# Handing the last attention heads to the output gate in SBUF instead of through DRAM, in a two-layer encoder trunk on one core

## The chip, the core and the metric

The kernel runs on one core of one Trainium2 chip. Its engines work through queues of their own: PE (TensorE, matrix multiplies; its weight loads are listed as PEld), DVE (VectorE), ACT (ScalarE), POOL (GpSimd) and SP (SyncE, which here only issues DMAs; its rows in a timeline read SPq). Each engine takes its instructions in the order in which they were written, and waits for another engine or a DMA where the program put a semaphore. The metric is the device time of one execution in microseconds, as the median of several executions.

## The reference

An input x of 512 tokens by 1024 features goes through two layers. A layer normalizes x and projects it into queries, keys and values of its own mixer (8 heads of 128; in the first layer a dilated window attention with three dilations, in the second a grouped-query attention), queries of 4 memory heads, and a gate of 12 x 128 columns. The 12 head results are multiplied by the gate's SiLU and go through an output projection that is added to x:

```python
def reference(x, mem, ...):
    for i in range(DEPTH):                       # DEPTH = 2
        h = rmsnorm(x, norm_g[i])
        mem_h = rmsnorm(mem, mem_norm_g[i])
        if i % 2 == 0:
            proj = h @ w_in_a[j]
            o_mix = mixer_dilated(qkv, qn_a[j], kn_a[j], ang_a)          # 8 heads
        else:
            proj = h @ w_in_b[j]
            o_mix = mixer_axial_gqa(q, k, v, qn_b[j], kn_b[j], ang_b)    # 8 heads
        o_mem = memory_attention(q_mem, mem_h, w_mem_kv[i], ...)         # 4 heads
        o = concat([o_mix, o_mem])
        x = x + (o * silu(gate)) @ w_out[i]
```

## The kernel before

All matrix products work on split numbers: a weight piece of 128 x 1024 is loaded (`wl`, L246, issued by SP), in part summed with others by accumulating DMAs that POOL issues (L260 to L279), cast to its high part `wh` by ACT (L295) and to its low part `wo` by DVE (L305), and the products high x high, high x low and low x high go through PE at L170, L171 and L174 into the PSUM bank `pj`. Many of the large products are built from seven smaller ones (`s_chunk`): ACT or DVE takes each bank into a tile `sn` (L372 keeps it, L383 takes a difference, L389 adds), and finished quarters go to a caller's `ev`.

The order is written by a small driver. A "slot" passes with each chunk of weights; generators (attention heads, evacuations, preparations) are resumed when their slot is due, and each writes a few instructions into the engines' queues. The order on each engine is thus fixed when the program is built.

A finished head result is a tile `o` of 128 x 512 out of the pool `s2` (14 buffers that take turns). `attn_a` (first layer) and `attn_b` (second) hand it to `put_od` (L1002) or `put_ob` (L1295), which write it to the DRAM tile `od` or `odb` by a DMA on SP and note the head in `o_done`. `gates` makes the gate's columns with `s_chunk` in three groups: memory heads (g = 0), heads 0 to 3 (g = 1) and heads 4 to 7 (g = 2). Its `ev` gets a quarter: two heads by 256 tokens, 128 x 512. It writes the tanh (ACT), the SiLU's product (L787), waits for slots until both heads are in `o_done`, issues a load `og` of both heads' 256 tokens (L780), waits one more slot and multiplies: into `yf` at L795 (g < 2), or in place at L798 (g = 2). For g = 2 ACT then casts the high part of `y` (L801) and DVE takes the low part (L803), on which the products of `out_rest` work. Heads 6 and 7 make the last two quarters of each layer.

The output projection has a first part, again through `s_chunk`, whose results POOL adds to the residual with an accumulating DMA `acc<-sn` (L876, two halves), and a second part, `out_rest`, whose banks DVE adds to the same `acc` (L756), which hence waits for these DMAs. In the first layer the finished rows are then written to DRAM as `x1d` (L1254, SP) and normalized for the second layer (L482); the rotation tables `tbraw` and `grB` are loaded behind those writes in SP's queue (L1273, L1275) and used by DVE at L1279 and L1282. In the same stretch the memory tokens `m` of the second layer are normalized (ACT L475, POOL L477/L436/L437, DVE L482).

Of the kernel before, what the change touches and what calls it, by code (L numbers as in the profile page):

```python
# [13 lines left out]
ALU = mybir.AluOpType  # L14
# [10 lines left out]
BULK, ACTIVE, SET_AT, WARM, MEM_B, PREP_Y, ACC_AT, PREP_B, HALF, SET_B = 2, 2, 15, 1, 12, 1, 4, 1, {"a": 3, "b": 3, "o": 0}, 1  # L25
MEM_STEP = 1, 1
MEM_D = 4
PD = 2
EO = 2, 2, 1, 2, 2, 1
YB = {"m": (2, 2), "k": (1, 1, 1), 0: (1, 2, 1), 1: (1, 2, 1)}  # L30
# [95 lines left out]
def trunk_kernel(ctx: ExitStack, tc: tile.TileContext, x, mem, wall, norm_g, mem_norm_g, gcol,  # L126
                 qn_a, kn_a, qn_b, kn_b, ident_d, mask_d, tab_a, tab_b, out):
    nc = tc.nc
    V, A, G, T = nc.vector, nc.scalar, nc.gpsimd, nc.tensor
# [8 lines left out]
    def big(dt=F32, name="big"):  # L138
        return pool.tile([128, 2048], dt, tag="big", name=name, bufs=NBIG)

    def m4(dt=F32, name="m4"):
        return pool.tile([128, 1024], dt, tag="m4", name=name, bufs=NM4)

    def s2(dt=F32, name="s2"):
        return pool.tile([128, 512], dt, tag="s2", name=name, bufs=NS2)
# [321 lines left out]
    def norm_1(xb, both=False):  # L467

        ss = sm(2, "ss")
        for j in range(2):  # L470
            jk = s2(name="sq")
            if both and j:
                V.tensor_tensor_reduce(jk, xb[j], xb[j], 1.0 / 1024.0, 0.0, ALU.mult, ALU.add, ss[:, j:j + 1])
            else:
                A.activation(jk, xb[j], AF.Square, scale=1.0 / 32.0, accum_out=ss[:, j:j + 1])  # L475
        r, e = sm(1, "rstd"), sm(1, "mse")
        G.tensor_tensor(e, ss[:, 0:1], ss[:, 1:2], ALU.add)  # L477
        return rstd_of(e, 1)
# [113 lines left out]
    def halves(t):  # L592
        return [t[:, 0:512], t[:, 512:1024]]
# [17 lines left out]
    def mem_norm(layer):  # L611
# [4 lines left out]
        t = [halves(v) for v in t]  # L616
        yield MEM_D
        n = [norm_1(t[0])]
# [142 lines left out]
            chunk(1, 4, group, ev)  # L761


    def gates(od, o_done):

        ys, yf, y_done, YW = [None] * 4, [None, None], set(), {}

        def gate(H, first, g, half=False):


            yt = [[m4(F32R, "y").rearrange("p (h t) -> p h t", h=2) for _ in range(2)] for _ in range(2)] if g == 2 else None
            if g < 2:
                yf[g] = [m4(name="yf") for _ in range(2)]

            def ev(q, u, t):
                i, j = int(q[0]) - 1, int(q[1]) - 1
                h0, ts = first + 2 * j, slice(i * 256, (i + 1) * 256)
                def load():
                    o = s2(name="og")
                    nc.sync.dma_start(o.rearrange("p (h t) -> p h t", h=2), od[h0:h0 + 2, :, ts].rearrange("h p t -> p h t"))  # L780
                    return o

                o = load() if {h0, h0 + 1} <= o_done else None
                th = s2(name="th")
                A.activation(th, t, AF.Tanh, scale=0.5)
                yield 1
                V.scalar_tensor_tensor(t, th, 1.0, t, ALU.add, ALU.mult)  # L787
                yield 1
                if not o:
                    while not {h0, h0 + 1} <= o_done:  # L790
                        yield 1
                    o = load()
                    yield 1
                if g < 2:
                    V.tensor_tensor(yf[g][j][:, i * 512:(i + 1) * 512], t, o, ALU.mult)  # L795
                    y_done.add((g, i, j))
                    return
                V.tensor_tensor(t, t, o, ALU.mult)  # L798
                yield 1
                tv = t.rearrange("p (h t) -> p h t", h=2)  # L800
                A.copy(yt[j][0][:, :, ts], tv)  # L801
                yield 1
                V.tensor_tensor(yt[j][1][:, :, ts], tv, yt[j][0][:, :, ts].bitcast(F32), ALU.subtract)  # L803
                y_done.add((g, i, j))
                if {(2, 0, j), (2, 1, j)} <= y_done:
                    for k in range(2):
                        ys[2 * j + k] = (yt[j][0][:, k], yt[j][1][:, k])

            s_chunk(256, H, ev, tokens=False, half=half, soon=g == 2)

        def prep_y():

            def wait(*gi):
                while not {(g, i, j) for g, i in gi for j in range(2)} <= y_done:
                    yield 1

            def put(k, src):
                t = big(F32R, "y" + k)
                for j in range(2):
                    js = slice(j * 512, (j + 1) * 512)  # L820
                    lo = t[:, 1024 + j * 512:1024 + (j + 1) * 512]
                    A.copy(t[:, js], src[j])
                    V.tensor_tensor(lo, src[j], t[:, js].bitcast(F32), ALU.subtract)
                YW[k] = t.rearrange("p (a k t) -> p a k t", a=2, k=4)

            while None in yf:
                yield 1
            a11, a21, a12, a22 = [[yf[g][j][:, i * 512:(i + 1) * 512] for j in range(2)] for g in range(2) for i in range(2)]
            yield from wait((1, 0))
            put("12", a12)  # L830
            yield 1
            yield from wait((0, 0))
            put("11", a11)
            yield 1
            yield from wait((0, 1), (1, 1))
            s1 = [s2(name="ys") for _ in range(2)]
            for j in range(2):
                V.tensor_tensor(s1[j], a21[j], a22[j], ALU.subtract)
            yield 1
            put("S1", s1)  # L840
            yield 1
            for j in range(2):
                V.tensor_tensor(s1[j], s1[j], a11[j], ALU.subtract)
            yield 1
            put("S2", s1)
            yield 2
            for j in range(2):
                V.tensor_tensor(a12[j], a12[j], s1[j], ALU.add)
            yield 1
            put("S4", a12)  # L850
            yield 1
            for j in range(2):
                V.tensor_tensor(a21[j], a11[j], a21[j], ALU.subtract)
            yield 1
            put("S3", a21)
            yield 2
            put("22", a22)

        return gate, prep_y, YW, ys
# [52 lines left out]
    def prep():  # L912

        n = {}
        for c in range(5):
            if c < 4:
                n[c] = norm_1(xb[c])
            if c:
                norm_2(xb[c - 1], n[c - 1], rows["x"])
            if 1 < c < 4:  # L920
                first_t(H, xb[c - 2], c - 2)
            yield 1
        for c in range(2):
            yield from diffs_t(H, xb[2 + c], c)
            drv.spawn(rest_t(H, c, (2, 2, 2)), 1)
            yield 1

    def setup():

        nc.sync.dma_start(mask, mask_d)  # L930
        nc.sync.dma_start(tabA, tab_a.rearrange("p (b c d) -> p b c d", b=2, c=4))
        nc.sync.dma_start(grA[:, 0:3], qn_a[0:1, :, 0:32].to_broadcast([128, 3, 32]))
        nc.sync.dma_start(grA[:, 3:6], kn_a[0:1, :, 0:32].to_broadcast([128, 3, 32]))
        yield 4
        V.tensor_tensor(gk, gc[:, 0:3], gc[:, 3:6], ALU.mult)
        V.tensor_scalar(gk, gk, QS, None, ALU.mult)
        V.tensor_scalar(gc[:, 6:8], gc[:, 6:8], QS, None, ALU.mult)
        V.memset(gk[0:32, :], 1.0)
        V.tensor_scalar(grA[:, 0:3], grA[:, 0:3], QS, None, ALU.mult)
        yield 1  # L940
        for cs_ in range(2):
            G.tensor_tensor(ropeA[:, cs_], tabA[:, cs_, :, None, :].to_broadcast([128, 4, 6, 32]),
                            grA[:, None].to_broadcast([128, 4, 6, 32]), ALU.mult)
            yield 1
# [35 lines left out]

    drv.spawn(prep(), PD)
    drv.spawn(setup(), SET_AT)
# [11 lines left out]
    s_chunk(512, H, ev_v0)  # L994

    od = dram.tile([12, 128, S], F32, name="od", bufs=1)
    o_done = set()

    def put_od(i, t=None):
        if t is None:  # L1000
            return s2(name="o")
        nc.sync.dma_start(od[i], t)  # L1002
        o_done.add(i)

# [70 lines left out]
    def attn_a(h, qk0, qs, ks, v12, n_done):  # L1075
# [91 lines left out]

        pts = {}
        rs = put_od(h)

        def scale(o):
# [62 lines left out]
        pv(0)  # L1234
        yield 2
        put_od(h, rs)

    gate, prep_y, YW, ys = gates(od, o_done)
    for c in A_ORDER:
        if c.isdigit():  # L1240
            drv.later(attn_a(int(c), *head_chunk(int(c))))
# [45 lines left out]
    drv.spawn(setup_b(), SET_B)  # L1287

    od_b = dram.tile([12, 128, S], F32, name="odb", bufs=1)
    o_done_b = set()  # L1290

    def put_ob(i, t=None):
        if t is None:
            return s2(name="o")
        nc.sync.dma_start(od_b[i], t)  # L1295
        o_done_b.add(i)

# [142 lines left out]
    for kvh in range(2):  # L1440
# [9 lines left out]
        if kvh == 0:  # L1450
            drv.later(attn_b())

    gate, prep_y, YW, ys = gates(od_b, o_done_b)
    gate(H2, 8, 0, HALF.get("m"))
    gate(H2, 0, 1, HALF.get("a"))
    drv.spawn(prep_y(), PREP_B)
# [118 lines left out]
```

## Time and profile before

| | before |
|---|---|
| median of 3 runs | 966.98 us (965.21 to 967.11) |
| profiled execution | 968.3 us |
| its span, first to last instruction | 966.5 us |
| mean granted TensorE clock | 0.996 |
| PE busy | 946.8 us (98%) |
| DVE busy | 791.4 us (82%) |
| ACT busy | 681.7 us (71%) |
| POOL busy | 341.4 us (35%) |

The profile is of one execution, 1.8 us of which lie outside the span; it took 1.3 us more than the median. Starts are counted from the span's begin. In a timeline a row gives start, duration in all, engine, line, operation, output and input with their shape, how many instructions it stands for, and in brackets how long the engine was idle before it and what ended that. On DVE the durations of neighbours overlap, so the distance of two starts says more than the durations. The first layer ends and the second begins at about 590 to 690 us; the second layer's last gate lies at about 930 to 943 us.

### The profile page before, as it was taken

How to read it: one execution, taken by the hardware profiler on the slowest of the kernel's cores; microseconds unless marked ns; L12 is line 12 of the kernel's file. 1: busy time of each engine (PE TensorE's matmuls, PEld its weight loads, DVE VectorE, ACT ScalarE, POOL GpSimd, SP SyncE). 2: the span in 40 equal slices, each digit the busy share in tenths (PEclk: the TensorE clock that was granted, in tenths of full speed). 3: DMA queues.
4: the chain of work that ended last, by engine and by line, in shares of the span. 5: the costliest groups of instructions: out<-in, count | busy, mean ns of one | idle time of the engine just before them, and what ended most of it. 6: DMA issues, size and time to landing. Idle time of an engine off the chain costs nothing.

```text
span 966.5 us, 16604 instructions
## 1 busy us (share of the span) xinstructions
PE 946.8 (98%) x5682; PEld 833.2 (86%) x5682; DVE 791.4 (82%) x1411; ACT 681.7 (71%) x1701; POOL 341.4 (35%) x482
## 2 busy tenths in 40 slices
PE   8999999999999999999999999999899999999998
PEld 5879888888888888888899997788899999998886
DVE  5898676878888888888888999769878898769883
ACT  5775689686868686868685657546768977879770
POOL 1512423557554545454726011322332330111010
PEclk9999999999999999999999999999899999999999
DMA  9989956969686868685959889889766687777744
GB/s 360 317 235 327 271 116 172 294 120 268 149 258 143 262 150 258 154 261 132 283 132 241 266 206 297 268 242 366 167 157 129 199 235 179 207 204 190 206 131 131
DMA packets 89129, 209.81 MB, mean 217 GB/s; under 512 B 25298, under 2 KB 36050, under 8 KB 89044
## 3 DMA queue, kind: packets, MB, share of 16 engines
q1 hardware_dynamic: 69892, 145.76, 43.4%
q0 software_dynamic: 17856, 60.83, 33.4%
q10 hardware_dynamic: 1296, 2.16, 0.6%
q8 instruction: 45, 0.74, 0.3%
q14 instruction: 40, 0.33, 0.1%
HBM read 157.27 MB, written 12.65 MB: 176 GB/s over the span
## 4 chain that ended last, share of the span: by engine, by line
PE 80%; DVE 8%; DMA 6%; ACT 3%; issue 2%; POOL 1%; SPq 0%; DVEq 0%; POOLq 0%; ACTq 0%
PE pj L170 21%; PE pj L171 21%; PE pj L174 20%; DVE wo L305 2%; PE qT L585 2%; PE sa L1106 1%; PE oo L1208 1%; PE pt L1187 1%; PE sa L1102 1%; PE ptb L1405 1%; DMA og<-odb 1%; DMA acc<-sn 1%; DMA wl<-wl 1%; DMA grB<-in_qn_b_dram 1%; DMA od<-o 1%
## 5 line engine op out<-in xcount | busy, mean ns | idle before, releaser
L305 DVE TENSOR_TENSOR wo<-wl,wh 128x1024 fp32r<-128x1024 f32 x255 | 315.1, 1242 | 6.0 <-ACT wh L295 5.8
L295 ACT CAST wh<-wl 128x1024 fp32r<-128x1024 f32 x255 | 268.5, 1060 | 29.3 <-PE pj L171 18.9
L170 PE MATMUL pj<-wh,hS 128*128 128x512 f32 (+1 forms) x448 | 159.0, 368 | 3.9 <-DVE sn L389 3.9
L171 PE MATMUL pj<-wh,hS 128*128 128x512 f32 (+1 forms) x448 | 153.6, 356 | 0.0
L170 PE MATMUL pj<-wh,h 128*128 128x512 f32 (+1 forms) x336 | 117.9, 365 | 0.0
L171 PE MATMUL pj<-wh,h 128*128 128x512 f32 (+1 forms) x336 | 114.0, 353 | 0.0
L437 POOL TENSOR_TENSOR rstd<-mse,half 128x4 f32<-128x4 f32 (+2 forms) x98 | 103.1, 1052 | 8.2
L174 PE MATMUL pj<-wo,hS 128*128 128x512 f32 (+1 forms) x448 | 100.8, 355 | 2.0 <-DVE wo L305 2.0
L170 PEld LDWEIGHTS pj<-wh,hS 128*128 128x128 f32 x448 | 85.9, 192 | 14.8 <-issue 2.6
L171 PEld LDWEIGHTS pj<-wh,hS 128*128 128x128 f32 x448 | 86.1, 192 | 10.3
L372 ACT COPY sn<-pj 128x512 f32<-128x512 f32 x132 | 73.1, 590 | 29.7 <-PE pj L174 29.7
L436 POOL TENSOR_SCALAR mse<-hss 128x4 f32<-128x4 f32 (+1 forms) x86 | 45.1, 525 | 132.2 <-ACT junk L573 128.0
L174 PEld LDWEIGHTS pj<-wo,hS 128*128 128x128 f32 x448 | 75.3, 191 | 14.5 <-DVE wo L305 2.7
L573 ACT ACTIVATE junk<-sn 128x128 f32<-128x128 f32 x264 | 79.1, 308 | 4.1 <-DVE sn L383 4.1
L1050 POOL TENSOR_TENSOR ta<-sn,tabs 128x128 f32<-128x128 f32 (+1 forms) x64 | 37.4, 592 | 118.6 <-DVE sn L578 92.0
L389 DVE TENSOR_TENSOR sn<-pj,sn 128x512 f32<-128x512 f32 x99 | 67.7, 686 | 12.3 <-PE pj L174 11.8
L174 PE MATMUL pj<-wo,h 128*128 128x512 f32 (+1 forms) x336 | 74.8, 352 | 0.0
L171 PEld LDWEIGHTS pj<-wh,h 128*128 128x128 f32 x336 | 63.8, 190 | 7.4
L170 PEld LDWEIGHTS pj<-wh,h 128*128 128x128 f32 x336 | 63.6, 189 | 7.4 <-DVE sn L389 0.2
L279 POOL DMA_DIRECT2D wl<-wl x33 | 29.1, 881 | 111.9 <-DVE wo L305 56.0
L174 PEld LDWEIGHTS pj<-wo,h 128*128 128x128 f32 x336 | 56.0, 189 | 8.7
L578 DVE TENSOR_TENSOR sn<-sn,rstd 128x512 f32<-128x512 f32 (+1 forms) x82 | 48.0, 594 | 7.2 <-POOL rstd L437 7.2
(235 smaller groups left out, 2335.1 us busy)
## 6 DMA issues: line engine op xcount, KB each, us to landing
wl<-in_wall_dram SPq DMA_DIRECT2D x222, 512.0 KB, 7.0
wl<-wl POOLq DMA_DIRECT2D x66, 512.0 KB, 5.5
wl<-in_wall_dram POOLq DMA_DIRECT2D x42, 512.0 KB, 8.5
acc<-sn POOLq DMA_DIRECT2D x16, 256.0 KB, 4.8
od<-o SPq DMA_DIRECT2D x12, 256.0 KB, 5.6
og<-od SPq DMA_DIRECT2D x12, 256.0 KB, 5.5
odb<-o SPq DMA_DIRECT2D x12, 256.0 KB, 3.4
og<-odb SPq DMA_DIRECT2D x12, 256.0 KB, 4.2
```

The source lines that it names most:

```text
L170: T.matmul(o, a, b, start=start, stop=False, skip_group_check=True)
L171: T.matmul(o, c, d, start=False, stop=False, skip_group_check=True)
L174: T.matmul(o, a, b, start=False, stop=stop, skip_group_check=True)
L295: A.copy(wh, self.tile[self.items[i]])
L305: V.tensor_tensor(wo, self.tile[key], wh.bitcast(F32), ALU.subtract)
L372: A.copy(t, b)
L389: V.tensor_tensor(t, b, t, ALU.subtract if q == "12" else ALU.add)
L436: G.tensor_scalar(e, ss, EPS, None, ALU.add)
L437: G.tensor_tensor(r, e, half[:, 0:n], ALU.pow)
L573: A.activation(jk, p[:, j * 128:(j + 1) * 128], AF.Square, scale=QS, accum_out=ss[:, j:j + 1])
L578: V.tensor_tensor(xn[:, 0:n], p.rearrange("p (a b) -> p a b", a=4)[:, 0:n], r[:, 0:n, None].to_broadcast([128, n, 128]), ALU.mult)
L1050: G.tensor_tensor(ta[:, 0:n], xn[:, 0:n, 0:32], ropeA[:, 0, b, s0:s0 + n], ALU.mult)
```

## The change

The tile `o` of head 7 in the first layer and of heads 6 and 7 in the second is not written to DRAM. `put_od` and `put_ob` only note it in `o_here`, and the gate reads it from there. The gate's `ev` collects its two heads one by one: a head in `o_here` is taken as it is, and the partner of such a head that is in DRAM (head 6 of the first layer) gets a load of its own of 128 x 256. Where a quarter has such a head, the multiplication is made in two instructions, one for each head. A head that goes this way keeps its buffer of the pool until the multiplication.

```diff
+DIRECT, DIRECT_B = (7,), (6, 7)
...
-    def gates(od, o_done):
+    def gates(od, o_done, o_here, direct):
...
+                hs, got = (h0, h0 + 1), {}
+                tv = t.rearrange("p (h t) -> p h t", h=2)
                 def load():
-                    o = s2(name="og")
-                    nc.sync.dma_start(o.rearrange(...), od[h0:h0 + 2, :, ts]...)
-                    return o
-                o = load() if {h0, h0 + 1} <= o_done else None
+                    if "o" not in got and all(h in o_done for h in hs):
+                        ...                       # one load for both heads, as before
+                    for n, h in enumerate(hs):
+                        if h in got:
+                            continue
+                        if h in o_here:
+                            got[h] = o_here[h][:, None, ts].to_broadcast([128, 2, 256])
+                        elif h in o_done and (hs[1 - n] in direct):
+                            o = s2(name="og")[:, 0:256]
+                            nc.sync.dma_start(o, od[h, :, ts])
+                            got[h] = o[:, None, :].to_broadcast([128, 2, 256])
+                def times(dst):
+                    if "o" in got:
+                        V.tensor_tensor(dst, t, got["o"], ALU.mult)
+                    else:
+                        dv = dst.rearrange("p (h t) -> p h t", h=2)
+                        for n, h in enumerate(hs):
+                            V.tensor_tensor(dv[:, n], tv[:, n], got[h][:, n], ALU.mult)
+                load()
                 th = s2(name="th")
                 A.activation(th, t, AF.Tanh, scale=0.5)
...
-                if not o:
-                    while not {h0, h0 + 1} <= o_done:
+                if not all(h in got for h in hs):
+                    load()
+                    while not all(h in got for h in hs):
                         yield 1
-                    o = load()
-                    yield 1
+                        load()
+                    if not all(h in o_here for h in hs):
+                        yield 1
...
-                V.tensor_tensor(t, t, o, ALU.mult)
+                times(t)
...
     def put_od(i, t=None):
         if t is None:
             return s2(name="o")
+        if i in DIRECT:
+            o_here[i] = t
+            return
         nc.sync.dma_start(od[i], t)
         o_done.add(i)
...                                   # put_ob likewise, with DIRECT_B and o_here_b
```

The order on PE and on POOL stays as it was. In the changed kernel the lines behind the first of these edits have higher numbers: the load of both heads is at L785, that of one head at L794, the multiplication of both at L799, that of one at L803, the casts of `y` at L824 and L826, `put_od`'s write at L1028.

On DVE, at the end of the first layer (`o` is head 7's result, `og` what was loaded, `m` the memory tokens), this stands before:

```order
L1220 TENSOR_TENSOR o<-oo,o 128x512
L389 TENSOR_TENSOR sn<-pj,sn 128x512
L305 TENSOR_TENSOR wo<-wl,wh 128x1024
L389 TENSOR_TENSOR sn<-pj,sn 128x512
L305 TENSOR_TENSOR wo<-wl,wh 128x1024 x3
L798 TENSOR_TENSOR sn<-sn,og 128x512 x2
L383 TENSOR_TENSOR sn<-sn 128x512 x2
L803 TENSOR_TENSOR y<-sn,y 128x2x256 x2
L389 TENSOR_TENSOR sn<-pj,sn 128x512 x2
```

and this now:

```order
L1246 TENSOR_TENSOR o<-oo,o 128x512
L390 TENSOR_TENSOR sn<-pj,sn 128x512
L306 TENSOR_TENSOR wo<-wl,wh 128x1024
L390 TENSOR_TENSOR sn<-pj,sn 128x512
L306 TENSOR_TENSOR wo<-wl,wh 128x1024 x3
L803 TENSOR_TENSOR sn<-sn,og 128x256
L803 TENSOR_TENSOR sn<-sn,o 128x256
L803 TENSOR_TENSOR sn<-sn,og 128x256
L803 TENSOR_TENSOR sn<-sn,o 128x256
L384 TENSOR_TENSOR sn<-sn 128x512 x2
L826 TENSOR_TENSOR y<-sn,y 128x2x256 x2
L390 TENSOR_TENSOR sn<-pj,sn 128x512 x2
```

Nothing moved here: the two multiplications became four of half the width at the same place, and every other one of them reads head 7's tile itself.

On SP, in the last part of the first layer (`row` a norm's weights, `v` and `oth` pieces of the attention), this stands before:

```order
L1144 DMA oth<-ds 128x4x2
L598 DMA row<-in_norm_g_dram 128x1024
...
L780 DMA og<-od 128x2x256
L868 DMA acc<-in_x_dram 128x1024 x4
L246 DMA wl<-in_wall_dram 128x1024 x6
L598 DMA row<-in_mem_norm_g_dram 128x1024
L615 DMA m<-in_mem_dram 128x1024 x2
L1002 DMA od<-o 128x512
L246 DMA wl<-in_wall_dram 128x1024
L780 DMA og<-od 128x2x256 x2
L246 DMA wl<-in_wall_dram 128x1024 x8
L1254 DMA x1d<-acc 128x512 x4
```

and this now:

```order
L1170 DMA oth<-ds 128x4x2
L794 DMA og<-od 128x256
L599 DMA row<-in_norm_g_dram 128x1024
...
L794 DMA og<-od 128x256
L785 DMA og<-od 128x2x256
L891 DMA acc<-in_x_dram 128x1024 x4
L247 DMA wl<-in_wall_dram 128x1024 x6
L599 DMA row<-in_mem_norm_g_dram 128x1024
L616 DMA m<-in_mem_dram 128x1024 x2
L247 DMA wl<-in_wall_dram 128x1024 x9
L1280 DMA x1d<-acc 128x512 x4
```

The write of head 7 and the two loads of heads 6 and 7 are gone from between the weight loads, and two loads of head 6 alone stand some twenty rows further ahead, the first of them ahead of a norm's weights, the second ahead of the load of heads 4 and 5.

On DVE at the end of the second layer this stands before:

```order
L389 TENSOR_TENSOR sn<-pj,sn 128x512
L305 TENSOR_TENSOR wo<-wl,wh 128x1024 x2
L798 TENSOR_TENSOR sn<-sn,og 128x512 x2
L305 TENSOR_TENSOR wo<-wl,wh 128x1024
L383 TENSOR_TENSOR sn<-sn 128x512 x2
L803 TENSOR_TENSOR y<-sn,y 128x2x256 x2
```

and this now:

```order
L390 TENSOR_TENSOR sn<-pj,sn 128x512
L306 TENSOR_TENSOR wo<-wl,wh 128x1024
L803 TENSOR_TENSOR sn<-sn,o 128x256 x4
L306 TENSOR_TENSOR wo<-wl,wh 128x1024 x2
L826 TENSOR_TENSOR y<-sn,y 128x2x256 x2
L384 TENSOR_TENSOR sn<-sn 128x512 x2
```

Here both heads come from SBUF, no slot is waited for a load, and the four multiplications and the low parts of `y` stand one weight piece and one difference earlier. SP's two writes and two loads of this place are gone.

More of the change, by code (lines that the diff above doesn't have):

```diff
@@ L777, in ev @@
                 h0, ts = first + 2 * j, slice(i * 256, (i + 1) * 256)
+                hs, got = (h0, h0 + 1), {}
+                tv = t.rearrange("p (h t) -> p h t", h=2)
                 def load():
-                    o = s2(name="og")
-                    nc.sync.dma_start(o.rearrange("p (h t) -> p h t", h=2), od[h0:h0 + 2, :, ts].rearrange("h p t -> p h t"))
-                    return o
-                o = load() if {h0, h0 + 1} <= o_done else None
+                    if "o" not in got and all(h in o_done for h in hs):
+                        o = got["o"] = s2(name="og")
+                        nc.sync.dma_start(o.rearrange("p (h t) -> p h t", h=2), od[h0:h0 + 2, :, ts].rearrange("h p t -> p h t"))
+                        got[h0] = got[h0 + 1] = o.rearrange("p (h t) -> p h t", h=2)
+                    for n, h in enumerate(hs):
[15 more added lines that the diff above has]
+                load()
                 th = s2(name="th")
@@ L788, in ev @@
                 yield 1
-                if not o:
-                    while not {h0, h0 + 1} <= o_done:
+                if not all(h in got for h in hs):
+                    load()
+                    while not all(h in got for h in hs):
                         yield 1
-                    o = load()
-                    yield 1
+                        load()
+                    if not all(h in o_here for h in hs):
+                        yield 1
                 if g < 2:
-                    V.tensor_tensor(yf[g][j][:, i * 512:(i + 1) * 512], t, o, ALU.mult)
+                    times(yf[g][j][:, i * 512:(i + 1) * 512])
                     y_done.add((g, i, j))
                     return
-                V.tensor_tensor(t, t, o, ALU.mult)
+                times(t)
                 yield 1
-                tv = t.rearrange("p (h t) -> p h t", h=2)
                 A.copy(yt[j][0][:, :, ts], tv)
@@ L996, in trunk_kernel @@
     od = dram.tile([12, 128, S], F32, name="od", bufs=1)
-    o_done = set()
+    o_done, o_here = set(), {}
     def put_od(i, t=None):
@@ L1236, in attn_a @@
         put_od(h, rs)
-    gate, prep_y, YW, ys = gates(od, o_done)
+    gate, prep_y, YW, ys = gates(od, o_done, o_here, DIRECT)
     for c in A_ORDER:
@@ L1289, in trunk_kernel @@
     od_b = dram.tile([12, 128, S], F32, name="odb", bufs=1)
-    o_done_b = set()
+    o_done_b, o_here_b = set(), {}
     def put_ob(i, t=None):
@@ L1294, in put_ob @@
             return s2(name="o")
+        if i in DIRECT_B:
+            o_here_b[i] = t
+            return
         nc.sync.dma_start(od_b[i], t)
@@ L1451, in trunk_kernel @@
             drv.later(attn_b())
-    gate, prep_y, YW, ys = gates(od_b, o_done_b)
+    gate, prep_y, YW, ys = gates(od_b, o_done_b, o_here_b, DIRECT_B)
     gate(H2, 8, 0, HALF.get("m"))
```

## The prediction

> **What bounds the kernel now.** I read the page's busy times first, then what PE waits for, then the chain that ended last, and then the engines' timelines around PE's gaps.
>
> ```profile
> PE 946.8 (98%) x5682; PEld 833.2 (86%) x5682; DVE 791.4 (82%) x1411; ACT 681.7 (71%) x1701; POOL 341.4 (35%) x482
> ```
>
> PE is busy for 946.8 of 966.5 us. The change takes no matmul away, so it can gain only where PE stands still or runs at a low clock. PE's waits from 600 us to the end:
>
> ```profile
> PE pj L170 <- DVE sn L389: 3.2, 2, 2.5
> PE pj L174 <- DVE wo L305: 1.8, 1, 1.8
> PE xT L488 <- DVE acc L482: 1.3, 1, 1.3
> PE xT L488 <- issue: 0.7, 1, 0.7
> ```
>
> Here stand the total, the count and the longest. PE's timeline puts the three long ones, 1.3 + 1.8 + 2.5 = 5.6 us, into the start of the second layer, and DVE ends each:
>
> ```profile
> 664.57 1.06 PE L488 MATMUL xT<-ident,acc 128*128 128x128 f32 x8 [1.32 <-DVE acc L482]
> 681.56 1.22 PE L174 MATMUL pj<-wo,hS 128*128 128x256 f32 x8 [1.81 <-DVE wo L305]
> 685.25 0.55 PE L170 MATMUL pj<-wh,hS 128*128 128x256 f32 x1 [2.47 <-DVE sn L389]
> ```
>
> So from 664 to 685 us the kernel runs at DVE's pace. The chain says what DVE's pace hangs on: ahead of 650 us it goes through two DMAs, and from there by DVE nearly without a break to the last PE gap.
>
> ```profile
> 627.31 9.48 DMA acc<-sn
> ...
> 642.72 8.06 DMA grB<-in_qn_b_dram
> 684.50 0.61 DVE sn L389
> ```
>
> DVE's own timeline shows the same links, and ahead of them the wait that the change is about (in brackets the idle time before a row):
>
> ```profile
> 615.17 1.23 DVE L305 TENSOR_TENSOR wo<-wl,wh 128x1024 fp32r<-128x1024 f32 x1 [1.70 <-ACT wh L295]
> 618.25 1.38 DVE L798 TENSOR_TENSOR sn<-sn,og 128x512 f32<-128x512 f32 x2 [1.84 <-DMA og<-od]
> 619.54 1.29 DVE L383 TENSOR_TENSOR sn<-sn 128x512 f32<-128x512 f32 x2
> ...
> 636.89 0.69 DVE L756 TENSOR_TENSOR acc<-pj,acc 128x512 f32<-128x512 f32 x1 [3.21 <-DMA acc<-sn]
> ...
> 647.24 1.41 DVE L482 SCALAR_TENSOR_TENSOR acc<-acc,rstd,row 128x512 f32<-128x512 f32 x2
> 650.80 0.23 DVE L1279 TENSOR_SCALAR grB<-grB 128x128 f32<-128x128 f32 x1 [2.15 <-DMA grB<-in_qn_b_dram]
> ```
>
> **First layer: what the wait is worth.** SP issues the loads of heads 6 and 7 behind head 7's write:
>
> ```profile
> 613.51 1.37 SPq L780 DMA_DIRECT2D og<-od  x2
> 614.94 24.13 SPq L246 DMA_DIRECT2D wl<-in_wall_dram  x8
> ```
>
> In the changed kernel head 7 is in SBUF before DVE comes to the multiplication, and head 6's halves are loaded some 40 us ahead. DVE's wait of 1.84 us goes: the multiplications start at 618.25 - 1.84 = 616.41. What is late next there is DVE itself, since the `wo` piece at 615.17 had its own wait for ACT, which the change doesn't touch.
>
> The two multiplications of 128 x 512 take 619.54 - 618.25 = 1.29 us from start to start of the next group. Four of half the width replace them. The nearest rows for that width:
>
> ```profile
> L578 DVE TENSOR_TENSOR sn<-sn,rstd 128x256 f32<-128x256 f32 x32 | 12.7, 417 | 0.0
> 588.94 1.14 DVE L1174 TENSOR_SCALAR p<-p,c 128x256 f32<-128x256 f32 x4
> ```
>
> Four by 417 ns are 1.67 us if nothing overlaps; the four of L1174 took 1.14 us in all. So the split costs between 1.1 - 1.3 = -0.2 and 1.7 - 1.3 = +0.4 us. I take 0, the side of the four that ran in a row, which these will do too. [...]
>
> So DVE is done with the gate 1.8 us earlier. Both things behind it follow. POOL's accumulating DMAs wait for DVE's L383 and stand in POOL's queue around the memory tokens' norm, which waits for ACT, which waited for the multiplication:
>
> ```profile
> 618.97 1.30 ACT L801 CAST y<-sn 128x512 fp32r<-128x512 f32 x2 [2.53 <-DVE sn L798]
> 620.82 1.76 POOL L876 DMA_DIRECT2D acc<-sn  x2 [8.38 <-DVE sn L383]
> 626.65 1.85 POOL L876 DMA_DIRECT2D acc<-sn  x2
> ```
>
> The second pair at 626.65 moves to 624.8, and with it the landing at 627.31 + 9.48 = 636.79, DVE's L756 at 636.89, the `x1d` writes, the load of `grB` behind them in SP's queue, DVE at 650.80, and so PE's gaps: 1.8 us.
>
> One term can make it more. The last DMA of that pair took 9.48 us, and SP was issuing weight loads at the time (eight from 614.94 on, over 24 us). Put out earlier, it meets fewer of them, but it may also just wait for the same transfers: between nothing (or a little less than nothing) and several us. The cap comes from what is late next: if `grB` came sooner, DVE would still be at its L482 of 647.24 and free of it 2.15 us ahead of 650.80; that work moves only with PE's output, by the 0.7 us that PE waited (for "issue") in that stretch. Hence 2.15 + 0.7 = 2.85 us at most. Of the 1.0 us between 1.84 and that cap I take a little under half, 0.45 us, since I can't tell which end is nearer. The first layer's part is 1.84 + 0.45 = 2.3 us, with ends at 1.4 (split at its dearest, no relief) and 2.9.
>
> Nothing takes it back later: PE can follow, since its gaps of 5.6 us are more than twice as long, and the view of PE's waits has no DMA among its reasons after 600 us.
>
> **First layer: SP.** Head 7's write and two loads no longer stand among the weight loads. Those behind them may start earlier, but no PE wait names a weight load, so that is worth 0. If it did harm, it would be by taking DMA time from `acc<-sn`, which is in the term above. Head 6's two loads were moved the other way, and they are a rival below.
>
> **First layer: the pool.** Head 7's tile keeps its buffer until 617 us instead of the end of its write. The next taker comes out of the same 14 in turn, and the multiplication frees it earlier than it freed the `og` tiles before. Worth 0.
>
> **Second layer.** DVE's wait for the loads, 2.48 us, goes as well, and two writes and two loads. But here PE doesn't wait for DVE. From 912.6 us to the last instruction its only wait is this one, which ends right at the stretch's beginning, far ahead of this gate:
>
> ```profile
> PE pj L170 <- DVE sn L389: 0.7, 1, 0.7
> ```
>
> ```profile
> 937.72 1.37 DVE L798 TENSOR_TENSOR sn<-sn,og 128x512 f32<-128x512 f32 x2 [2.48 <-DMA og<-odb]
> ...
> 941.34 1.29 DVE L803 TENSOR_TENSOR y<-sn,y 128x512 fp32r<-128x512 f32 x2
> 942.46 1.07 PE L174 MATMUL pj<-wh,y 128*128 128x512 f32 x4
> ```
>
> PE comes to the low parts at 942.46, and DVE's first one is done by then. So this half of the change is worth 0, and its reordering can't cost either while DVE has 2.48 us to spare.
>
> **The sum.** 1.84 + 0.45 + 0 = 2.3 us: 968.3 - 2.3 = 966.0 us for an execution like the profiled one, which lay 1.3 us above the median, and 966.98 - 2.3 = **964.7 us** as the median.
>
> **The rivals.**
>
> The gain is swallowed. `acc<-sn` lands when the DMA engines are through with what is queued, not when it was issued, so the landing stays near 636.8, and the chain behind it too.
>
> ```profile
> acc<-sn POOLq DMA_DIRECT2D x16, 256.0 KB, 4.8
> ```
>
> For it: 9.48 us for 256 KB, beside weight loads; against it: the usual one of these DMAs lands in half that time. Time: 966.98, within 0.2%, which is 1.9 us and about what a measurement of this kernel can tell from no change.
>
> The clock changes phase. After the gap at 685.25 PE ran slowly for five microseconds:
>
> ```profile
> 685.60 0.41 PE L171 MATMUL pj<-wh,hS 128*128 128x256 f32 x1
> 685.81 0.41 PE L170 MATMUL pj<-wh,hS 128*128 128x256 f32 x1
> 690.46 0.28 PE L171 MATMUL pj<-wh,hS 128*128 128x256 f32 x1
> 690.58 0.29 PE L170 MATMUL pj<-wh,hS 128*128 128x256 f32 x1
> 685.00:691.00 6.00, 5.75 (x30) 5.78 (x31) 5.31 (x7) 2.66 (x11) 3.62 (x2) 0.57 0.35 115
> ```
>
> (The last row is a stretch: PE busy, PEld, DVE, ACT, POOL, then the granted clock, 0.57.) Starts were 0.21 us apart instead of 0.12, over 24 matmuls 24 x 0.09 = 2.2 us. With gaps that begin 2 us earlier or are shorter this can fall away: 2.3 + 2.2 = 4.5 us, 962.5. [...]
>
> Slower: head 6's early load holds SP up. The place is SP's queue at 567 us, behind `oth`:
>
> ```profile
> 567.06 3.30 SPq L598 DMA_DIRECT2D row<-in_norm_g_dram  x1
> ...
> 574.38 0.38 SPq L780 DMA_DIRECT2D og<-od  x1
> 561.86 7.57 DMA od<-o
> 588.34 0.69 DVE L798 TENSOR_TENSOR sn<-sn,og 128x512 f32<-128x512 f32 x1
> ```
>
> The load reads what head 6's write puts down, and that write lands at 561.86 + 7.57 = 569.43. SP, which would be at 567.06, waits 2.4 us, and behind it stand a norm's weights, weight loads, `v`, the load of heads 4 and 5 and four of `acc`; head 6's second half adds another 128 KB ahead of that load. The load of heads 4 and 5 is issued at 574.38, and at the 11.0 us that the DMA list gives as the median of this stretch it lands at 585.4, 2.9 us before DVE multiplies at 588.34.
>
> ```profile
> og<-od SPq DMA_DIRECT2D x2, 256.0 KB, 11.0
> 560.00:595.00 35.00, 33.32 (x199) 28.82 (x198) 34.16 (x55) 21.88 (x33) 5.98 (x7) 1.00 0.98 254
> ```
>
> The DMA engines are 98% busy there (next to last number) and DVE 34.16 of 35 us, so a later landing has no cover beyond these 2.9 us. The shift is from 0 (SP's 3.3 us for `row` may be the same waiting) to 2.4 us and the time of head 6's 256 KB at 254 GB/s, 1.0 us: 3.4. That would stall DVE 0.5 us and leave a gain of 1.8. For a loss the landing must come over 2.9 + 2.3 = 5.2 us later, by weight and `acc` loads that overtake it; each us beyond that is a us lost. At twice my upper shift, 6.8 us, it is 1.6 us slower: 968.6.
>
> That the second layer's part, half of the change, does nothing is my forecast already.
>
> **How the numbers follow.** Forecast (gain 1.4 to 2.9): 0.53, of which 0.10 ends within 0.2%. Clock: 0.12. Swallowed, or cut below 1.9 us by SP: 0.20. Slower: 0.15, of which 0.02 stays within 0.2%. Faster 0.43 + 0.12 = 0.55; same 0.10 + 0.20 + 0.02 = 0.32; slower 0.13. The range leaves out about a tenth on each side: from 962.4, which takes in the clock case's 962.5, to 967.8, halfway from no change to the slower rival's 968.6.
>
> **What would show it.** Right: no DVE wait for `og` in the first layer, `acc<-sn` of the second pair issued near 624.8 and landed near 634.5, `grB` used near 648.5, PE's last gap ending near 683. Wrong: the issue earlier but the landing at 636.8 (swallowed); a DVE wait for the load of heads 4 and 5 near 588 (slower); no low clock behind the last gap (clock); a second-layer tail that is longer or shorter than before.

## The result

The changed kernel takes 964.9 us (median of 22 runs, 962.83 to 968.33), the kernel before 967.24 us in the same comparison (22 runs). The ratio is 0.9969, 95% interval 0.9959 to 0.998: a gain of 3.0 us, between 1.9 and 4.0. By the medians it is 2.3 us, by the means 2.9: the kernel before has more long executions, two of them above 972 us, and a median doesn't see these. Disturbed runs, of which the experiments below have one of 1978.12 us in `e5` and one of 1032.56 us of the kernel before beside `e5` to `e8`, are left out of the ratios and not of the medians. The forecast was 2.3 us and 964.7 us.

### The profile page after: what moved, and what is told of

Same layout as the page of the kernel before. It is cut to its first block, busy times and chain, and to the rows that moved or that the text cites. A ratio compares the mean times of both kernels' runs of the same rounds, so it can differ in the third digit from the quotient of the medians.

```text
span 963.8 us, 16603 instructions
## 1 busy us (share of the span) xinstructions
PE 946.6 (98%) x5682; PEld 834.1 (87%) x5682; DVE 791.4 (82%) x1415; ACT 681.9 (71%) x1701; POOL 343.0 (36%) x482
## 4 chain that ended last, share of the span: by engine, by line
PE 84%; DVE 8%; DMA 4%; ACT 3%; issue 2%; DVEq 0%; ACTq 0%
PE pj L171 22%; PE pj L172 22%; PE pj L175 22%; DVE wo L306 2%; PE qT L586 2%; PE oo L1234 1%; PE sa L1132 1%; PE pt L1213 1%; PE sa L1128 1%; PE ptb L1434 1%; DMA og<-odb 1%; DMA x1d<-acc 1%; DMA od<-o 1%; PE row L607 1%; PE ob L175 1%
## 5 line engine op out<-in xcount | busy, mean ns | idle before, releaser
L172 PEld LDWEIGHTS pj<-wh,hS 128*128 128x128 f32 x448 | 86.1, 192 | 10.2
```

Of the source, the lines that this page charges most:

```text
L172: T.matmul(o, c, d, start=False, stop=False, skip_group_check=True)
```

## The profile after

Its span is 963.8 us against 966.5. Of PE's waits from 600 us to the end these are left (total, count, longest):

```profile
PE pj L171 <- DVE sn L390: 3.0, 2, 2.5
PE pj L175 <- DVE wo L306: 1.1, 1, 1.1
PE ob L175 <- DVE pbT L1443: 0.6, 1, 0.6
```

Gone are the wait of 1.3 us for `acc` at 664 us, and the two of 0.7 and 0.2 us for "issue" and for the low part of `y`, which lay right behind the gate. The DVE timeline at the gate and at the links behind it:

```profile
589.82 0.69 DVE L799 TENSOR_TENSOR sn<-sn,og 128x512 f32<-128x512 f32 x1
...
616.66 1.23 DVE L306 TENSOR_TENSOR wo<-wl,wh 128x1024 fp32r<-128x1024 f32 x1 [1.72 <-ACT wh L296]
617.80 0.42 DVE L803 TENSOR_TENSOR sn<-sn,og 128x256 f32<-128x256 f32 x1
618.13 0.42 DVE L803 TENSOR_TENSOR sn<-sn,o 128x256 f32<-128x256 f32 x1
...
619.14 1.29 DVE L384 TENSOR_TENSOR sn<-sn 128x512 f32<-128x512 f32 x2
...
636.16 0.69 DVE L757 TENSOR_TENSOR acc<-pj,acc 128x512 f32<-128x512 f32 x1 [3.03 <-DMA acc<-sn]
...
644.04 0.69 DVE L757 TENSOR_TENSOR acc<-pj,acc 128x512 f32<-128x512 f32 x1 [2.03 <-PE pj L175]
...
648.32 0.22 DVE L1305 TENSOR_SCALAR grB<-grB 128x128 f32<-128x128 f32 x1
```

The first row says how the two executions must be laid side by side: the same instruction stood at 588.34 before. This execution was thus 1.5 us late when it came to the place of the change, for reasons that lie ahead of it. From there on it gained: the multiplications start 0.45 us earlier than before by the clock of the span, so 1.9 us by this measure; `acc` of L757 is taken 0.7 us earlier (2.2); `grB` is used 2.5 us earlier (4.0), with no wait in brackets. POOL's second pair of accumulating DMAs:

```profile
626.25 1.85 POOL L899 DMA_DIRECT2D acc<-sn  x2
```

And SP at the place of the slower rival, then the DMA list for the stretch in which the load of heads 4 and 5 is issued:

```profile
568.39 0.85 SPq L1170 DMA_DIRECT2D oth<-ds  x1
574.23 0.32 SPq L794 DMA_DIRECT2D og<-od  x1
...
580.11 0.54 SPq L785 DMA_DIRECT2D og<-od  x1
```

```profile
og<-od SPq DMA_DIRECT2D x1, 256.0 KB, 9.2
```

SP stood from 569.24 to 574.23, 5.0 us, and what ended that was head 6's write. The load of heads 4 and 5 was issued at 580.11 and took 9.2 us: 589.3, half a microsecond before DVE used it at 589.82, without a wait.

## The experiments

Three questions: which half of the change works, and by which of its effects; by which path the gain reaches the end; what the early loads and the second layer take from it. Ratios are to the kernel before, each with its 95% interval.

### Which half

`e1_first_only`:

```diff
-DIRECT, DIRECT_B = (7,), (6, 7)
+DIRECT, DIRECT_B = (7,), ()
```

> The changed kernel with the first layer's half alone: DIRECT = (7,), DIRECT_B = (). Theory (the whole gain is the first layer's, since PE never waits for DVE in the second layer's last gate): as the changed kernel, 2.3 to 3 us under the kernel before, about 964.5 us. Rival (the second layer's wait of 2.48 us on DVE also counts): the gain splits, this run lies 1 us or more above the changed kernel, about 966. Profile: no DVE wait for og near 617 us, the wait for odb of about 2.5 us near 935 us back, PE without a gap there.

Measured: 964.97 us, ratio 0.9972 (0.9958 to 0.9986), the whole gain as far as these runs can tell. At the second layer's last gate (925 to 950 us) DVE waits for `odb` again:

```profile
DVE sn L799 <- DMA og<-odb: 2.7, 1, 2.7
```

`e2_second_only`:

```diff
-DIRECT, DIRECT_B = (7,), (6, 7)
+DIRECT, DIRECT_B = (), (6, 7)
```

> The changed kernel with the second layer's half alone: DIRECT = (), DIRECT_B = (6, 7). Theory: no change, 966.5 to 967.5 us, with DVE's wait for odb near 935 us gone and PE's tail as long as before. Rival (the second layer counts): 1 us or more faster than before, about 966 or less.

Measured: ratio 1.0008 (0.9993 to 1.0022), so between 0.7 us faster and 2.1 us slower than the kernel before. The median, 969.1 us, lies above the 966.5 to 967.5 that were expected; why is open. The rival, a gain of 1 us or more, is out: the second layer's half brings nothing. A wait of 2.5 us on DVE was taken away where PE had work.

This run showed something else, which the kernel before's profile had hidden. In its first layer, which is that of the kernel before, DVE's timeline reads:

```profile
620.02 1.38 DVE L799 TENSOR_TENSOR sn<-sn,og 128x512 f32<-128x512 f32 x2 [2.68 <-DMA og<-od]
...
646.06 0.69 DVE L757 TENSOR_TENSOR acc<-pj,acc 128x512 f32<-128x512 f32 x1 [2.03 <-PE pj L175]
...
650.35 0.22 DVE L1305 TENSOR_SCALAR grB<-grB 128x128 f32<-128x128 f32 x1
```

and PE's, right behind the gate:

```profile
621.42 0.50 PE L171 MATMUL pj<-wh,y 128*128 128x512 f32 x1 [0.60 <-ACT y L824]
...
623.25 0.73 PE L175 MATMUL pj<-wh,y 128*128 128x512 f32 x2 [0.17 <-DVE y L826]
...
627.46 0.63 PE L489 MATMUL xT<-ident,m 128*128 128x128 f32 x4 [0.73 <-issue]
```

Here DVE doesn't wait for `grB` at all. It waits 2.03 us for PE's last bank of `out_rest`, and PE is late because it had itself waited 0.60 + 0.17 + 0.73 = 1.5 us for what comes out of the gate. The wait of 2.03 us is no sign of this execution: it stands there in all fourteen profiles, the kernel before's at 644.29. So DVE comes to this bank ahead of PE in all of them, and behind it the gate can be felt only through PE or through a DMA.

How late PE is can be read between two groups of its matmuls, the one that begins at 617.91 in the kernel before and the last of `out_rest`; first the kernel before, then the changed one:

```profile
617.91 1.07 PE L174 MATMUL pj<-wo,y 128*128 128x512 f32 x4
...
643.18 1.07 PE L174 MATMUL pj<-wh,y 128*128 128x512 f32 x4
```

```profile
619.39 1.07 PE L175 MATMUL pj<-wo,y 128*128 128x512 f32 x4
...
642.94 1.07 PE L175 MATMUL pj<-wh,y 128*128 128x512 f32 x4
```

That is 25.27 and 23.55 us. The same distance in the five profiles in which the first layer's gate waits for its load `og`, and in the nine in which it doesn't (e4, e9 and e10 come further down):

| profile | DVE's wait for `og`, us | PE from group to group, us | more than 23.55 |
|---|---|---|---|
| before | 1.84 | 25.27 | 1.72 |
| e4 | 1.91 | 25.33 | 1.78 |
| e10 (two waits) | 2.42 | 25.87 | 2.32 |
| e9 | 2.65 | 26.13 | 2.58 |
| e2 | 2.68 | 26.11 | 2.56 |
| the nine others | none | 23.54 to 23.55 | 0 |

PE thus loses DVE's wait, less about 0.1 us, in every one of these executions, the kernel before's among them. The brackets show only part of it (0.20 + 0.69 in the kernel before), as it counts from the listed end of a matmul (these start 0.23 us apart and are listed with 0.39), and as the first ones behind a stand took longer: from L488's eight matmuls at 625.69 to the next group it was 1.09 us, in the changed kernel 0.79.

There are then two paths from the gate to PE's later gaps: this one, straight through PE, and the predicted one by way of `grB`, which is the last only where `grB` lands late.

### Which effect

`e3_traffic_kept` is `e1` with head 7's write and both loads of heads 6 and 7 issued at their old place as well, into tiles that nobody reads, so that DVE doesn't wait for them. Head 6's two early loads are there too:

```diff
         if i in DIRECT:
             o_here[i] = t
+            nc.sync.dma_start(od[i], t)
             return
...
+                    if any(h in direct for h in hs):
+                        spare = s2(name="spare")
+                        nc.sync.dma_start(spare..., od[h0:h0 + 2, :, ts]...)      # read by nobody
```

> First layer's half alone, but head 7 is also written to DRAM and both loads of heads 6 and 7 are still issued at their old place, into tiles that nobody reads; SP's queue there is that of the kernel before, only DVE doesn't wait for it. (Head 6's two early loads are there too.) Theory (it is DVE's wait that counts): as with the first layer's half alone, about 964.5 us. Rival (what counts is that SP's queue and the DMA engines are rid of the write and the loads, so that weight loads run ahead and acc<-sn and grB land sooner): the gain falls to 1 us or less, 966 us or more; in between, the part of each can be read from the landing of acc<-sn and from whether DVE waits for grB.

Measured: 964.66 us, ratio 0.9967 (0.9951 to 0.9983). The whole gain is there, with the write and both loads in SP's queue at their old place:

```profile
609.88 0.33 SPq L1030 DMA_DIRECT2D od<-o  x1
610.25 0.42 SPq L247 DMA_DIRECT2D wl<-in_wall_dram  x1
614.61 1.57 SPq L818 DMA_DIRECT2D spare<-od  x2
```

```profile
617.31 0.42 DVE L803 TENSOR_TENSOR sn<-sn,og 128x256 f32<-128x256 f32 x1
...
635.96 0.69 DVE L757 TENSOR_TENSOR acc<-pj,acc 128x512 f32<-128x512 f32 x1 [3.06 <-DMA acc<-sn]
```

So it is DVE's wait, and neither the traffic nor the weight loads behind it. POOL's second pair stood at 625.77 here, and the last of it was used 635.96 - 625.77 = 10.2 us later. That distance is 10.2 us in the kernel before as well (626.65 to 636.89), and 9.9 us in the changed one (626.25 to 636.16), without the traffic.

### By which path

`e4_tables_early` and `e5_after_tables_early` load the tables early, in the kernel before and in the changed one:

```diff
+    def tables():
+        if not tabs_b:
+            ...                                       # tbraw, grB and their loads, moved here
     def ev_o(n, b, x1):
+        if (n, b) == (0, 2):
+            tables()
         if n:
```

> The kernel before, with the loads of grB and tbraw issued ahead of the first x1d writes in SP's queue instead of behind them (about 3.5 us sooner). Theory (the last link ahead of PE's gaps is DVE's wait for grB, 2.15 us, behind which DVE is free at 648.65): that wait goes, DVE still waits 1.8 us for og, and the kernel is about 2 us faster, 965. Rival (grB's wait is no link, what is late next comes at the same time, such as the L482 that waits for acc): 967, as before.

Measured: 966.35 us, ratio 0.9986 (0.9973 to 1.0): 0.9 us by the medians and 1.4 by the ratio, of the 2 us that were expected, and the interval reaches to no gain. DVE takes `grB` without a wait, at about the time of e2, and the wait for `og` and PE's waits behind the gate are still there:

```profile
650.11 0.22 DVE L1289 TENSOR_SCALAR grB<-grB 128x128 f32<-128x128 f32 x1
```

> The changed kernel with grB and tbraw loaded early as in e4: the fourth corner of a square with the kernel before, the changed kernel and e4, where grB is out of the way in both. Theory A, as predicted (the gain came through acc<-sn, x1d and grB to DVE): with grB early that path is cut, and this run should lie where e4 lies, 966.4. Theory B, formed from the profiles of e2 and e4 (DVE didn't wait for grB there, but for PE's banks of out_rest; what the change closes are PE's own waits for the gate at 621 to 627 us, 0.60 + 0.17 + 0.73 = 1.5 us): 1.5 to 1.9 us under e4, 964.5 to 964.9, and about 0.9 us under the changed kernel or equal to it.

Measured: 966.33 us, ratio 0.9978 (0.9963 to 0.9993). That alone speaks for neither theory: the median is e4's, as theory A had it, the ratio lies between, and without its longest execution the median is 966.04 us. Its profile shows why it can't decide. PE's wait from 900 us to the end:

```profile
PE pj L171 <- DVE sn L390: 3.2, 1, 3.2
```

That wait, 0.7 us before and 0.5 us in the changed kernel, stands where DVE waits for the load of heads 4 and 5 of the second layer, which still go through DRAM. In this execution what was gained in the first layer was lost there.

So the square was repeated without that place. `e8_four_heads_second`, `e9_no_first_four_second`, `e10_tables_four_second` and `e11_tables_first_four_second` all have

```diff
+DIRECT, DIRECT_B = (7,), (4, 5, 6, 7)      # e8; e11 with the tables early
+DIRECT, DIRECT_B = (), (4, 5, 6, 7)        # e9; e10 with the tables early
```

> The changed kernel with heads 4 to 7 of the second layer handed over, DIRECT_B = (4, 5, 6, 7). PE's wait near 910 us (0.5 to 0.7 us, for a sum that stands behind the multiplication by heads 4 and 5 on DVE) should go with the wait for their load: 0.5 us faster than the changed kernel, 964.3. Rival: DVE is full there anyway and the wait stays, 964.9; or two more buffers held make the attention wait, 966 or more.

> DIRECT = (), DIRECT_B = (4, 5, 6, 7): the first layer as before, heads 4 to 7 of the second layer handed over in SBUF. It is e8 without the first layer's half, so that the second wait for a way through DRAM (heads 4 and 5 of the second layer, PE idle 0.2 to 3.2 us near 910 in the profiles so far) can't take anything back. Theory: 0.5 us under the kernel before, 966.7, and 1.5 to 2.5 us over e8, with PE's waits for the gate at 621 to 627 us (0.9 to 1.5 us in all) still there. Rival (the first layer's gain only shows because of the second layer's wait): e8's time, 964.6.

> As e9, with grB and tbraw loaded early: no late grB, no wait near 910; only the first layer's gate still waits for DRAM. Theory B: 0 to 1 us under e9, about 966; DVE's wait of 1.8 to 2.7 us for og near 617 us and PE's short waits behind it still there. Theory A (the predicted path through acc<-sn and grB is the only one): as e11.

> As e10, with the first layer's half of the change: e5 without the wait near 910 us. If e5 lost its gain there (3.15 us of PE in its profile), this run is 1.5 to 2 us under e10 and about 1.5 to 2 under e5, 964 to 964.5. If it lies at e10's time, the first layer's half works only through grB, and theory B falls. It is also the first candidate for a version faster than the changed kernel (964.9).

| heads 4 to 7 of the second layer in SBUF | tables late | tables early |
|---|---|---|
| first layer through DRAM | e9: 966.36 us, 0.999 (0.9978 to 1.0002) | e10: 966.37 us, 0.9986 (0.9973 to 0.9999) |
| head 7 of the first layer in SBUF | e8: 964.57 us, 0.9969 (0.9955 to 0.9982) | e11: 964.45 us, 0.997 (0.9958 to 0.9983) |

Down a column the medians differ by 1.8 and 1.9 us, across a row by 0.1 us at most. The intervals of the ratios overlap a little. But e10 and e11 were measured beside the same executions of the kernel before, and eight of e11's nine executions are below the fastest of e10's twelve, 964.98 us. So the first layer's half gives about the same with the tables late and early. PE's waits from 600 us to the end, e10 first, then e11:

```profile
PE pj L171 <- DVE sn L390: 2.5, 1, 2.5
PE pj L175 <- DVE wo L306: 1.4, 1, 1.4
PE pj L175 <- DVE y L826: 0.8, 1, 0.8
PE xT L489 <- issue: 0.7, 1, 0.7
PE ob L175 <- DVE pbT L1453: 0.5, 1, 0.5
```

```profile
PE pj L171 <- DVE sn L390: 2.5, 1, 2.5
PE pj L175 <- DVE wo L306: 1.1, 1, 1.1
PE ob L175 <- DVE pbT L1453: 0.5, 1, 0.5
```

What the first layer's half takes away here is 0.8 + 0.7 + 0.3 = 1.8 us of PE's waits, and the medians differ by 1.9 us. Theory A, one path by way of `grB`, falls; theory B, the path straight through PE, stands.

e9's profile shows the other path once more, in an execution in which `grB` took 8.0 us:

```profile
651.75 0.23 DVE L1305 TENSOR_SCALAR grB<-grB 128x128 f32<-128x128 f32 x1 [1.82 <-DMA grB<-in_qn_b_dram]
```

That e8 isn't faster than the changed kernel, though PE has no wait left from 890 us on in its profile, suggests that this wait costs little in most runs of the changed kernel.

### What the early loads cost, and a faster version

`e6_both_heads` is the changed kernel with `DIRECT = (6, 7)`; `e7_head6_later` leaves head 6's loads out of the first of the gate's two tries:

```diff
-                load()
+                if all(h not in direct for h in hs):
+                    load()
                 th = s2(name="th")
```

> The changed kernel with both heads handed over in the first layer as well, DIRECT = (6, 7): head 6's write and its two early loads, for which SP waited 5 us, are gone, and the four multiplications stand one weight piece earlier on DVE. Theory (the early loads cost nothing, since the load of heads 4 and 5 still landed 0.5 us before DVE used it, and PE has no wait left at the gate): 964.5 to 965, as the changed kernel. Rival (the loads ahead do cost in some executions): 0.5 to 1.5 us faster, 963.5 to 964.4. Other side: head 6's buffer, held for 50 us more, makes a later taker wait: 966 or more.

> The changed kernel, in which head 6's first load stands behind the norm's weights, v and the weight pieces in SP's queue, next to the load of heads 4 and 5, so that SP needn't wait for head 6's write at 569 to 574 us. The rest is the same. Theory (the early wait of SP cost nothing): 964.5 to 965, as the changed kernel. Rival (slower rival of the prediction in part: a late load of heads 4 and 5 takes some of the gain in part of the executions): 0.5 to 1 us faster.

Measured: e6 964.51 us, ratio 0.9973 (0.9959 to 0.9987); e7 964.21 us, ratio 0.9977 (0.996 to 0.9993). In e7's profile SP passes the place without that stand and issues the load of heads 4 and 5 at 575.12. Neither differs from the changed kernel by what these runs can tell. SP's stall of 5 us cost nothing that shows.

`e12_all_direct` puts everything together: `DIRECT, DIRECT_B = (6, 7), (4, 5, 6, 7)` and the tables early.

> As e11, with head 6 of the first layer handed over as well, DIRECT = (6, 7): everything that the runs point to in one kernel. Expected 0 to 0.5 us under e11, 963.5 to 964.5; other side: buffers of the pool held longer make a taker wait, 966.

Measured: 963.16 us, ratio 0.996 (0.9946 to 0.9974). It is the lowest median of the study, a little under the 963.5 to 964.5 that were expected; its interval overlaps that of the changed kernel (0.9959 to 0.998), so that it beats the changed kernel is likely and not shown.

## Why the prediction was right, point by point

**DVE's wait for the gate: 1.84 us forecast, 1.9 us measured.** The multiplications started right behind the `wo` piece that waits for ACT. e1 and e3 show that this wait alone carries the gain. But 1.84 us is the least of the five profiles that have the wait; they go up to 2.68 and come to 2.3 us on average, of which PE lost 2.2.

**The split: 0 forecast, with +0.4 as the dear end.** The four took 619.14 - 617.80 = 1.34 us against 1.29: 0.05 us. They start 0.33 us apart and last 0.42. By its duration one of them is dearer than half of a full-width multiplication (0.42 against 0.69 / 2 = 0.35 us), but little of that is left in a row: 0.33 us from start to start against 1.29 / 4 = 0.32.

**Relief of `acc<-sn`: 0.45 us forecast; there was none to speak of.** This is the term that was mis-sized. From POOL's issue to DVE's use it was 10.2, 9.9 and 10.2 us in the kernel before, the changed kernel and e3. In the twelve profiles with this wait it was 10.0 to 10.2 us with head 7 through DRAM and 9.9 to 10.2 without. The landing moved with the issue, which also disposes of the rival that the gain is swallowed there; but it didn't come any sooner behind it.

**The path: half right.** The chain of the kernel before's one profile went through `grB`, and I took the whole of PE's later gaps for its effect. The load of `grB` took 8.1 us in that execution and 8.0 in e9's, and DVE waited; in e2's it took 6.1 us, and DVE didn't. The other path, PE's own delay by `y` and by the memory tokens' norm, I used only as a cap, at 0.7 us. It was worth 1.72 us in the very profile that the forecast was read from, and up to 2.58 in others. So the cap of 2.85 us was wrong as well: what came behind `grB` moved by 4.0 us from that profile to the one after, of which 1.72 us are PE's and 2.15 the wait for `grB`. In how many executions `grB` is late, and so how much of the mean gain is its part, the runs don't show.

**The number: partly luck.** Both paths start at the gate and pass on DVE's wait nearly whole, so the size had to come out near that wait. That it came out at 2.3 us by the medians is luck: the wait was read from an execution in which it was short, and a relief that doesn't exist made up for it.

**The second layer: 0, as forecast** (e2). But that nothing takes the gain back later was too strong. It was read from what PE waits for, which names no DMA; in e5's profile PE stood 3.2 us for DVE, and DVE had stood 5.6 us for the load of heads 4 and 5. How often that happens is open.

**SP and the slower rival: the place right, the size too small.** SP stood for 5.0 us where the rival had up to 2.4, and the load of heads 4 and 5 was issued at 580.11 instead of 574.38, 4.2 us later when the 1.5 us by which this execution was late are taken off. It landed sooner after its issue, in 9.2 instead of 11.0 us, and so left DVE half a microsecond. The rival needed a shift of over 5.2 us for a loss.

**The clock: a part of the scatter, not of the gain.** The granted clock (the third number from the end) from 660 to 700 us in the changed kernel, then in e1, which differs from it only in the second layer:

```profile
660.00:700.00 40.00, 36.38 (x250) 0.91 0.88 253
```

```profile
660.00:700.00 40.00, 36.40 (x263) 0.96 0.86 249
```

PE's last two gaps are alike in both (1.1 and 2.5 us), but the stretch at a granted clock of 0.5, which begins within the second of them, lasts about 6.8 us in the first and 3.4 in the second (added up from the granted clock of stretches of 2 and 4 us). So the same code up to here runs with a long or a short dip. What decides which of the two an execution has, the runs don't show.

Which dip an execution had can be told from its mean clock, since in all fourteen profiles 0.996 goes with 0.91 in this stretch and 0.998 with 0.96. Of the changed kernel's 22 executions 13 have 0.996 (median 965.78 us) and 9 have 0.998 (963.63). Of the kernel before's 26 beside e9 to e12, 13 have 0.996 (968.00 us) and 12 have 0.998 (965.98); of the 30 beside e1 to e4, 15 (968.08) and 14 (966.97). Executions with the long dip are thus 1.1 to 2.2 us longer, but it isn't rarer in the changed kernel, and at like clock the kernels differ by 2.2 to 3.3 us. The clock rival's gain of 4.5 us didn't come.

## What to carry to other kernels

Where PE is at 98%, look for the wait whose end PE's own next gap hangs on: DVE's wait of some 2 us at the end of the first layer was worth about 2 us, and one of 2.5 us at the end of the second nothing. A chain from one profiled execution shows the path that was last in that execution; before a cost is put on a link such as a small load, look for the second path that ends at nearly the same time. What a wait cost PE is read best as the distance between the same two groups of matmuls in both kernels, as the idle times in brackets showed only about half of it here. And where a change moves a load ahead of others in one queue, price the landing of the write that it reads: here SP stood for 5 us, and half a microsecond of cover was left.

## What was not expected of the hardware

The second of a pair of accumulating DMAs of 256 KB was used 9.9 to 10.2 us after the pair's issue, with and without the weight loads of SP's queue shifted around it. A load of 64 KB that is broadcast to 128 partitions, `grB`, took two times with the same first layer. The DMA lists of the stretch in which it is issued, in the kernel before and in e2 (the last number is the time to landing):

```profile
grB<-in_qn_b_dram SPq DMA_DIRECT2D x1, 64.0 KB, 8.1
```

```profile
grB<-in_qn_b_dram SPq DMA_DIRECT2D x1, 64.0 KB, 6.1
```

In e10, where it stood ahead of the writes of `x1d`, it took 4.4 us. What makes it late in some executions and not in others stays open.
